# A two-layer hybrid decoder trunk: mixer gates and token shift on VectorE and ScalarE, weight tiles placed between dependent steps, and the down product's operands at another address

## The chip, the cores and the metric

The kernel runs on one core of a Trainium2 chip. The core has TensorE (PE, matrix products, with its weight loads shown apart as PEld), VectorE (DVE), ScalarE (ACT), GpSimd (POOL), and SyncE (SP), whose queue issues the DMAs here. Each engine works through its own instructions in a fixed order and waits on semaphores where an operand or a buffer is not ready. The metric is the device time of one execution in microseconds, as the median of several runs.

## The reference

Two decoder layers over 512 tokens of width 1024, float32, then a final RMSNorm. In each layer, with `n = RMSNorm(h)`:

```python
p = n @ w_in                                     # 1024 x 4256
p_rw = p_rw + (shift(p_rw) - p_rw) * mu_shift    # token shift of r, k, v, decay, iclr, gate columns
y_a = rwkv7_time_mix(p_rw) @ w_out_rwkv          # 8 heads x 64, delta-rule recurrence over tokens
y_b = mla(q_lat, kv_lat, k_pe) @ w_out_mla       # 8 heads, causal softmax, rotary key
h = h + (sigmoid(gate_a) * y_a + sigmoid(gate_b) * y_b) @ w_out
u_gate, u_val = split(RMSNorm(h) @ w_ffn_up)     # 2 x 2816
h = h + (gelu(causal_conv3(u_gate)) * u_val) @ w_ffn_down
```

The token shift takes, for each token, a mix of its own projection and the one of the token before it; for the first token the one before is zero.

## The kernel before

Activations lie with features on the 128 partitions and the 512 tokens along the free dimension. Every large product is computed to nearly float32 accuracy from two rounded parts: an operand is split into a high part (ACT, a copy that rounds) and a low part (DVE, the difference). `mm3` (lines 245 to 248) then multiplies high by high, high by low and low by high, so that a block of 128 x 128 weights takes three matmuls of 512 columns. `wtile` (line 250) makes one output tile of 128 features: eight blocks, 24 matmuls, for a product over 1024 features.

Weights come as one stream of units of eight blocks, in the order of use that `_stream` lays out on the host. `produce` loads a unit (SP), and `parts` splits it (L201 on ACT, L202 on DVE). There are two buffers each for the raw unit and its two parts, so a unit can be split only when PE is done with the unit two before it.

A layer goes through these stages:

1. *First projections.* The gate-lora and decay/iclr columns, two gate tiles (`GATES[5]`) and the lora products, `rgate_d`.
2. *Pair stage* (lines 469 to 580). `pair(p)` is a generator for two heads: it projects k, r, v (`shifted`), forms decays with a scan (L478 to L504), normalises the key (L508 to L518), builds the operands AR, BK and BKb, and computes the chunk matrices in two halves of four chunks each (L553 on PE, masked into AM by L556 on DVE; L561 transposes BKb). It yields between steps, and the loop after it runs steps of pair p, steps of pair p+1 and gate tiles in turn. PSUM holds five `m` tiles for these steps and three accumulators.
3. *Latents* of the attention (lines 597 to 625): four projections, two token sums, two inverse roots, and their broadcast to all partitions (`rsqrt_bc`: DVE, a power on POOL, a copy on ACT, four transposes on PE).
4. *A_ak V* (L633), then the *triangular inversion*: DVE transposes, 30 substitution steps of two DVE instructions (L648, L650), DVE transposes, and a join of blocks on PE (L663, L670).
5. *Chunk recurrence* (from line 677): eight chunks, each with three dependent groups of small matmuls on PE (L687, L696, L704) with DVE between them. After it in the program stand the six gates of `GATES[4]`.
6. *Attention*, the gated outputs, the merge, `w_out`, and the feed-forward part, whose up product reads operands from the `xop` pool and whose down product reads operands (`hid`) from the pool `ff`, where they lie behind seven `ft` tiles of 520 floats.

A gate tile before: ACT copies PSUM to `gg` (L433), POOL multiplies by `rstd` (L437), ACT takes tanh (L438), SP stores it to `gate_d`. A shifted tile before: POOL clears column 0 of `cur` (L417), DVE writes `cur = ps * rstd` from column 1 on (L418), POOL subtracts (L420), DVE multiplies by `mu` and adds (L421).

The order of instructions on each engine is set ahead of the run by a planner of the tile framework. It takes program order as priority, and its own estimates of durations; where it thinks an engine would wait, it draws later work forward, as far as that work's operands and its tile slots (by `tag` and `bufs`) allow. So the gates of `GATES[4]` and the attention's first projections appear in the trace within the inversion and the recurrence, though they are written behind them. Tile pools are placed one after another in SBUF, those with `side="right"` from the far end.

Of the kernel before, what the change touches and what calls it, by code (L numbers as in the profile page):

```python
# [73 lines left out]
def _blocks(w):  # L74
    """[K, M] -> [K/128 * M/128 blocks of 128 x 128], output tile by output tile."""
    k, m = w.shape
    return w.reshape(k // 128, 128, m // 128, 128).transpose(2, 0, 1, 3).reshape(-1, 128, 128)
# [10 lines left out]
GATES = (range(2, 4), range(4, 6), range(6, 8), range(8, 10), range(10, 16), range(0, 2))  # L88


# the last operands of w_out come late: its first tiles leave them to the end
# [4 lines left out]
def _stream(a, l):  # L96
    """All weights of one layer as blocks of 128 x 128 in the order of their use, 8 to a unit."""
# [11 lines left out]
    out.append(lora.reshape(128, 8, 128).transpose(1, 0, 2))  # L109
    for p in range(4):  # L110
        if p == 0:
            out.append(tiles(_W_IN_RWKV[2:5]))
        out.append(tiles(_W_IN_RWKV[5 + 3 * p:8 + 3 * p] + [_W_IN_GATE[i] for i in GATES[p]]))
# [22 lines left out]
# units of the last tile of the last product, which is taken in two halves of its tokens  # L136
# [22 lines left out]
def build(ctx, tc, x, pos, wst, vecd, constd, out):  # L159
# [36 lines left out]
    # ---- weight stream: units of 8 blocks, split into high and low parts ahead of their use  # L196
# [8 lines left out]
    def produce():  # L205
# [4 lines left out]
        if u >= NUNITS - HELD:  # L210
            # the operands' slots are free by then: these units stay
# [12 lines left out]
    class Blocks:  # L224
        """Hands out 128 x 128 weight blocks in stream order."""
# [33 lines left out]
    def split(pool, src, scale, tag, bufs=None):  # L259
        """src * scale -> exact high and low operands."""  # L260
# [16 lines left out]
    def rsqrt_bc(ps, n, eps, mul=None, out=None, pst=stat, js=range(4)):  # L277
        """ps[:, js] (sums by token, blocks of 128) -> (ps / n + eps) ** -0.5 on all partitions"""
# [5 lines left out]
        w = sm.tile([128, 512], F32, name="nw", tag="nsq", bufs=1)  # L284
        A.copy(w[:, c].rearrange("p (j n) -> p j n", n=128), v[:, 4 + a:4 + b, None].to_broadcast([128, b - a, 128]))
        pb = pst()
# [14 lines left out]
    class Norm:  # L301
        """Sums of squares over the features; add() takes them tile by tile."""
# [21 lines left out]
    # ---- rotary tables  # L324
# [23 lines left out]
    # ---- scratch in DRAM  # L348
# [6 lines left out]
    # derived vectors  # L355
    der = []

    def derive():
        for l in range(DEPTH):
            d = cp.tile([128, 24], F32, name=f"der{l}")  # L360
# [4 lines left out]
            V.tensor_scalar(d[:, 16:20], vc(l, "k_a", 0, 4), -0.5, 1.0, ALU.mult, ALU.add)  # L365
            der.append(d)
# [25 lines left out]
    def mixer(l, ops, nrm, wks):  # L392
        with ExitStack() as mx:
# [201 lines left out]
            with pool(name=f"ti{l}", bufs=2) as ti:  # L595
# [119 lines left out]
                for i in GATES[4]:  # L715
                    gate(i, ti)
# [252 lines left out]
```

## Time and profile before

| | |
|---|---|
| median of 3 runs | 1656.53 us (1648.63 to 1659.28) |
| span of the profiled execution | 1654.1 us |
| PE busy | 1593.0 us (96%), 9014 matmuls |
| DVE busy | 959.5 us (58%) |
| ACT busy | 645.2 us (39%) |
| POOL busy | 275.4 us (17%) |
| pair stage, layer 0 | 53.6 to 191.2 us |
| latents and inversion, layer 0 | 191.2 to 262.8 us |
| recurrence, layer 0 | 262.8 to 305.5 us |
| pair stage, layer 1 | 854 to 1004 us |

The profile is of one execution. The first instruction of the span starts it and the last ends it; the three runs were timed apart from it, so 1654.1 stands beside them as one more execution, 2.4 us under their median. A busy PE is not PE at its peak: matmuls overlap in the record, so their spacing is the time of a stretch without gaps over its count. A few matmul records can be missing. The stage boundaries were read from the order of PE's instructions.

### The profile page before, as it was taken

How to read it: one execution, taken by the hardware profiler on the slowest of the kernel's cores; microseconds unless marked ns; L12 is line 12 of the kernel's file. 1: busy time of each engine (PE TensorE's matmuls, PEld its weight loads, DVE VectorE, ACT ScalarE, POOL GpSimd, SP SyncE). 2: the span in 40 equal slices, each digit the busy share in tenths (PEclk: the TensorE clock that was granted, in tenths of full speed). 3: DMA queues.
4: the chain of work that ended last, by engine and by line, in shares of the span. 5: the costliest groups of instructions: out<-in, count | busy, mean ns of one | idle time of the engine just before them, and what ended most of it. 6: DMA issues, size and time to landing. Idle time of an engine off the chain costs nothing.

```text
span 1654.1 us, 22422 instructions
## 1 busy us (share of the span) xinstructions
PE 1593.0 (96%) x9014; PEld 1271.2 (77%) x9014; DVE 959.5 (58%) x1448; ACT 645.2 (39%) x987; POOL 275.4 (17%) x246
## 2 busy tenths in 40 slices
PE   8999989999999999999999998899999999999997
PEld 6877766668888888888877777766688888888886
DVE  6668885666546555533348669747565555554333
ACT  6334333573433333322234333336634433333222
POOL 2333212400211011100023332123003111110000
PEclk9999989999999999999999999899999999999998
DMA  5323312314423233233342222223244233323232
GB/s 201 111 88 104 102 65 71 116 46 136 145 90 102 90 101 97 95 110 113 108 146 96 83 83 96 71 73 95 69 141 128 88 98 95 102 89 102 90 102 78
DMA packets 57849, 166.09 MB, mean 100 GB/s; under 512 B 6416, under 2 KB 9616, under 8 KB 57744
## 3 DMA queue, kind: packets, MB, share of 16 engines
q1 hardware_dynamic: 57600, 164.48, 31.0%
q8 instruction: 71, 1.16, 0.3%
q14 instruction: 34, 0.28, 0.1%
q10 hardware_dynamic: 144, 0.16, 0.0%
HBM read 147.32 MB, written 17.30 MB: 100 GB/s over the span
## 4 chain that ended last, share of the span: by engine, by line
PE 85%; DVE 10%; issue 2%; ACT 1%; POOL 1%; DMA 1%; SPq 0%; POOLq 0%; DVEq 0%; ACTq 0%
PE acc L246 24%; PE acc L247 24%; PE acc L248 24%; DVE wlo L202 3%; PE sc L830 2%; PE po L848 2%; PE pt L841 1%; PE xy L696 1%; DVE X L644 1%; DVE tm L648 1%; DVE AM L653 1%; POOL nv L283 1%; DVE X L650 1%; PE m L553 1%; DVE z L485 1%
## 5 line engine op out<-in xcount | busy, mean ns | idle before, releaser
L246 PE MATMUL acc<-hi,whi 128*128 128x512 f32 (+1 forms) x1910 | 755.7, 396 | 5.3 <-ACT hi L267 5.3
L248 PE MATMUL acc<-hi,wlo 128*128 128x512 f32 (+1 forms) x1910 | 748.9, 392 | 1.9 <-DVE wlo L202 1.8
L247 PE MATMUL acc<-lo,whi 128*128 128x512 f32 (+1 forms) x1910 | 750.6, 393 | 0.0
L201 ACT CAST whi<-raw 128x1024 fp32r<-128x1024 f32 (+2 forms) x249 | 253.3, 1019 | 569.1 <-PE acc L247 530.5
L202 DVE TENSOR_TENSOR wlo<-raw,whi 128x1024 fp32r<-128x1024 f32 (+2 forms) x249 | 327.5, 1319 | 188.9 <-ACT whi L201 188.1
L246 PEld LDWEIGHTS acc<-hi,whi 128*128 128x128 f32 x1910 | 362.4, 190 | 82.1 <-ACT hi L267 5.3
L248 PEld LDWEIGHTS acc<-hi,wlo 128*128 128x128 f32 x1910 | 361.7, 189 | 80.6 <-DVE wlo L202 3.6
L247 PEld LDWEIGHTS acc<-lo,whi 128*128 128x128 f32 x1910 | 362.2, 190 | 74.3 <-issue 0.7
L920 POOL TENSOR_TENSOR c<-c,rstd 128x512 f32<-128x512 f32 x44 | 57.3, 1304 | 378.0 <-ACT c L919 378.0
L913 DVE TENSOR_TENSOR u<-acc,rstd 128x512 f32<-128x512 f32 x44 | 30.3, 691 | 99.9 <-PE acc L248 94.1
L922 DVE TENSOR_TENSOR c<-c,acc 128x512 f32<-128x512 f32 x44 | 30.2, 687 | 82.4 <-POOL c L920 82.4
L437 POOL TENSOR_TENSOR gg<-gg,rstd 128x512 f32<-128x512 f32 x32 | 52.0, 1625 | 121.2 <-ACT gg L433 121.2
L919 ACT ACTIVATE c<-c 128x512 f32<-128x512 f32 x44 | 27.6, 632 | 78.7 <-DVE c L918 78.7
L315 POOL TENSOR_TENSOR nacc<-nacc,nsq 128x512 f32<-128x512 f32 x14 | 25.1, 1790 | 197.6 <-ACT nsq L314 197.6
L283 POOL TENSOR_TENSOR nv<-nv,cst 128x4 f32<-128x4 f32 (+1 forms) x10 | 14.4, 1440 | 234.5 <-DVE nv L282 234.5
L418 DVE TENSOR_TENSOR cur<-acc,rstd 128x512 f32<-128x512 f32 x28 | 19.2, 691 | 47.9 <-PE acc L248 42.1
L830 PE MATMUL sc<-K,q 128*128 128x128 f32 (+3 forms) x128 | 45.3, 449 | 0.0
L836 ACT ACTIVATE P<-P,mn 128x128 f32<-128x128 f32 (+3 forms) x64 | 35.5, 556 | 16.7 <-DVE mn L833 12.9
L553 PE MATMUL m<-AR,BK 64*128 64x128 f32 x256 | 25.4, 324 | 17.3 <-DVE AM L556 17.3
L833 DVE CUSTOM_DVE_ANT_0 P<-sc,cst 128x128 f32<-128x128 f32 (+3 forms) x64 | 30.4, 482 | 16.6 <-PE pt L841 9.7
L438 ACT ACTIVATE gg<-gg 128x512 f32<-128x512 f32 x32 | 20.2, 632 | 45.4 <-POOL gg L437 45.4
L848 PEld LDWEIGHTS po<-PT,Vt 128*64 128x64 f32 x320 | 22.0, 136 | 20.7 <-issue 8.8
(232 smaller groups left out, 1499.9 us busy)
## 6 DMA issues: line engine op xcount, KB each, us to landing
raw<-in_w SPq DMA_DIRECT2D x238, 512.0 KB, 3.4
gate_d<-gg SPq DMA_DIRECT2D x32, 256.0 KB, 2.4
AM<-gate_d SPq DMA_DIRECT2D x16, 256.0 KB, 4.1
gb<-gate_d SPq DMA_DIRECT2D x16, 256.0 KB, 3.7
h<-in_x SPq DMA_DIRECT2D x8, 256.0 KB, 4.5
rgate_d<-gt SPq DMA_DIRECT2D x8, 256.0 KB, 2.6
bl_d<-rk SPq DMA_DIRECT2D x8, 256.0 KB, 2.0
bl<-bl_d SPq DMA_DIRECT2D x8, 256.0 KB, 2.7
```

What stands on the lines that cost most here:

```text
L201: A.copy(hi, r)
L202: V.tensor_tensor(lo, r, hi.bitcast(F32), ALU.subtract)
L246: PE.matmul(ps, w[0], xx[0], start=first, stop=False)
L247: PE.matmul(ps, w[0], xx[1], start=False, stop=False)
L248: PE.matmul(ps, w[1], xx[0], start=False, stop=last)
L283: G.tensor_tensor(v[:, 4 + a:4 + b], v[:, a:b], mhalf[:, a:b], ALU.pow)
L437: G.tensor_tensor(gg, gg, rstd, ALU.mult)
L553: PE.matmul(pA[hh][:, c * 128:c * 128 + 128], BK[64 * hh:64 * hh + 64, 4 * hf + c, :], AR[p][64 * hh:64 * hh + 64, 4 * hf + c, :], start=T ...
L830: PE.matmul(sp[:, 0:n], qs[hh][:, 128 * b:128 * b + 128], ks[hh][:, 0:n], start=True, stop=True)
L836: A.activation(P[:, 0:n], P[:, 0:n], AF.Exp, bias=mn[:, 0:1], scale=-1.0, accum_out=mn[:, 1:2])
L848: PE.matmul(po[64 * hh:64 * hh + 64, 128 * b:128 * b + 128], Vt[:, kb, 64 * hd:64 * hd + 64], PTs[hh][:, 128 * kb:128 * kb + 128], start=k ...
L920: G.tensor_tensor(cc, cc, rstd, ALU.mult)
```

## The change

- *Gates.* `gate` now has DVE write `gg = ps * rstd` straight from PSUM, then tanh and the store. The two early gates (`gate_raw`, `GATES[5]`) still copy on ACT, and multiply on DVE instead of POOL.
- *Token shift.* `cur` has 512 columns and no cleared one. ACT writes `o = cur * (1 - mu)`, with `1 - mu` held in 14 new columns of `der`; DVE then adds `mu * cur` of the token before to columns 1 to 511. `der` grows from 24 to 40 columns in each layer, 128 bytes for both.
- *Pair steps.* `pair` yields also behind k, and behind each half of the chunk matrices. Pair p+2's k (for p of 0 and 1) or a third gate (for p of 2 and 3) is put between the halves of pair p. `GATES` gives pairs 2 and 3 three gates instead of two, and the group of the recurrence four instead of six. `_stream` follows the new order.
- *Latents.* `rsqrt_bc` is cut into `rsqrt_tok` (through the copy on ACT) and `spread` (transposes and the final pass). Both token sums and both `rsqrt_tok` now come ahead of the A_ak V products, the two `spread` and the scaling of the key latent behind them. The copies go into tiles of their own.
- *Inversion.* One gate of `GATES[4]` is written between the substitution and the join; the other three remain behind the recurrence.
- *Feed-forward.* The `ft` tiles have 528 instead of 520 floats; the columns used are the same.

Comments and docstrings were dropped too; that part of the diff is left out.

```diff
-GATES = (range(2, 4), range(4, 6), range(6, 8), range(8, 10), range(10, 16), range(0, 2))
+GATES = (range(2, 4), range(4, 6), range(6, 9), range(9, 12), range(12, 16), range(0, 2))
...
+    out.append(tiles(_W_IN_RWKV[2:6]))
     for p in range(4):
-        if p == 0:
-            out.append(tiles(_W_IN_RWKV[2:5]))
-        out.append(tiles(_W_IN_RWKV[5 + 3 * p:8 + 3 * p] + [_W_IN_GATE[i] for i in GATES[p]]))
+        out.append(tiles(_W_IN_RWKV[6 + 3 * p:8 + 3 * p] + [_W_IN_GATE[i] for i in GATES[p]] + _W_IN_RWKV[8 + 3 * p:9 + 3 * p]))
...
     def rsqrt_bc(ps, n, eps, mul=None, out=None, pst=stat, js=range(4)):
+        return spread(rsqrt_tok(ps, n, eps, js), mul, out, pst, js)
+
+    def rsqrt_tok(ps, n, eps, js=range(4), pool=sm, tag="nsq"):
         v = sm.tile([128, 8], F32, name="nv", tag="nv", bufs=2)
         a, b = js[0], js[-1] + 1
         c = slice(128 * a, 128 * b)
         V.tensor_scalar(v[:, a:b], ps[:, a:b], 1.0 / n, eps, ALU.mult, ALU.add)
         G.tensor_tensor(v[:, 4 + a:4 + b], v[:, a:b], mhalf[:, a:b], ALU.pow)
-        w = sm.tile([128, 512], F32, name="nw", tag="nsq", bufs=1)
+        w = pool.tile([128, 512], F32, name="nw", tag=tag, bufs=1)
         A.copy(w[:, c].rearrange("p (j n) -> p j n", n=128), v[:, 4 + a:4 + b, None].to_broadcast([128, b - a, 128]))
+        return w
+
+    def spread(w, mul, out, pst, js=range(4)):
         pb = pst()
...
-            d = cp.tile([128, 24], F32, name=f"der{l}")
+            d = cp.tile([128, 40], F32, name=f"der{l}")
...
+            V.tensor_scalar(d[:, 20:34], vc(l, "mu", 0, 14), -1.0, 1.0, ALU.mult, ALU.add)
...
-                    cur = ta.tile([128, 513], F32, name="cur", tag="cur", bufs=2)
-                    G.memset(cur[:, 0:1], 0.0)
-                    V.tensor_tensor(cur[:, 1:513], ps, rstd, ALU.mult)
+                    cur = ta.tile([128, 512], F32, name="cur", tag="cur", bufs=2)
+                    V.tensor_tensor(cur, ps, rstd, ALU.mult)
                     o = ta.tile([128, 512], F32, name=name, tag="sh", bufs=6)
-                    G.tensor_tensor(o, cur[:, 0:512], cur[:, 1:513], ALU.subtract)
-                    V.scalar_tensor_tensor(o, o, vc(l, "mu", idx), cur[:, 1:513], ALU.mult, ALU.add)
+                    A.activation(o, cur, AF.Copy, scale=der[l][:, 20 + idx:21 + idx])
+                    V.scalar_tensor_tensor(o[:, 1:512], cur[:, 0:511], vc(l, "mu", idx), o[:, 1:512], ALU.mult, ALU.add)
                     return o
...
                 def gate(i, pool=ta):
-                    gate_end(i, gate_raw(pool))
+                    ps = wtile(ops)
+                    gg = pool.tile([128, 512], F32, name="gg", tag="gg", bufs=2)
+                    V.tensor_tensor(gg, ps, rstd, ALU.mult)
+                    gate_out(i, gg)
...
                 def gate_end(i, gg):
-                    G.tensor_tensor(gg, gg, rstd, ALU.mult)
+                    V.tensor_tensor(gg, gg, rstd, ALU.mult)
+                    gate_out(i, gg)
+
+                def gate_out(i, gg):
                     A.activation(gg, gg, AF.Tanh, scale=0.5)
                     nc.sync.dma_start(gate_d[i], gg)
...
                     k = shifted(2 + 3 * p, "k")
+                    yield
                     r = shifted(3 + 3 * p, "r")
...
                         A.copy(BT[p][:, 4 * hf:4 * hf + 4, :].rearrange("p c n -> p (c n)"), pB)
+                        yield
 
                 pairs = [pair(p) for p in range(4)]
-                next(pairs[0])
-                next(pairs[0])
+                for _ in range(3):
+                    next(pairs[0])
+                next(pairs[1])
                 for p in range(4):
                     if p < 3:
                         next(pairs[p + 1])
                     next(pairs[p])
-                    for i in GATES[p][:1]:
+                    gate(GATES[p][0])
+                    next(pairs[p])
+                    gate(GATES[p][1])
+                    if p < 3:
+                        next(pairs[p + 1])
+                    next(pairs[p])
+
+                    if p < 2:
+                        next(pairs[p + 2])
+                    for i in GATES[p][2:]:
                         gate(i)
                     next(pairs[p])
-                    for i in GATES[p][1:]:
-                        gate(i)
-                    if p < 3:
-                        next(pairs[p + 1])
-                    next(pairs[p], None)
...
-                ssq = sc()
-                tok_sums(ssq, sq[0])
-                rq = tl.tile([128, 512], F32, name="rq", bufs=1)
-                rsqrt_bc(ssq, 256.0, NORM_EPS, tabs[1], rq, sc)
-                ssq = sc()
-                tok_sums(ssq, sq[2])
-                rk = ti.tile([128, 512], F32, name="rk", bufs=1)
-                rsqrt_bc(ssq, 128.0, NORM_EPS, None, rk, sc)
...
+                ws = []
+                for i, (t, n) in enumerate(((sq[0], 256.0), (sq[2], 128.0))):
+                    ssq = sc()
+                    tok_sums(ssq, t)
+                    ws.append(rsqrt_tok(ssq, n, NORM_EPS, pool=ti, tag=f"nw{i}"))
...
+                rq = tl.tile([128, 512], F32, name="rq", bufs=1)
+                spread(ws[0], tabs[1], rq, sc)
+                rk = ti.tile([128, 512], F32, name="rk", bufs=1)
+                spread(ws[1], None, rk, sc)
...
+                gate(GATES[4][0], ti)
                 half = [(64, 64), (0, 128)]
...
-                for i in GATES[4]:
+                for i in GATES[4][1:]:
                     gate(i, ti)
...
-                    u = fp.tile([128, 520], F32, name="u", tag="ft", bufs=7)
+                    u = fp.tile([128, 528], F32, name="u", tag="ft", bufs=7)
...
-                    c = fp.tile([128, 520], F32, name="c", tag="ft", bufs=7)
+                    c = fp.tile([128, 528], F32, name="c", tag="ft", bufs=7)
```

More of the change, by code (lines that the diff above doesn't have):

```diff
@@ L611, in mixer @@
                 G.tensor_tensor(sq[0], sq[0], sq[1], ALU.add)
-                ssq = sc()
-                tok_sums(ssq, sq[0])
-                rq = tl.tile([128, 512], F32, name="rq", bufs=1)
-                rsqrt_bc(ssq, 256.0, NORM_EPS, tabs[1], rq, sc)
-                ssq = sc()
-                tok_sums(ssq, sq[2])
-                rk = ti.tile([128, 512], F32, name="rk", bufs=1)
-                rsqrt_bc(ssq, 128.0, NORM_EPS, None, rk, sc)
-                V.scalar_tensor_tensor(lat[2], lat[2], vc(l, "kv_norm"), rk, ALU.mult, ALU.mult)
-                kp = tl.tile([128, 512], F32, name="kp", bufs=1)
-                k2 = ti.tile([128, 512], F32, name="k2", bufs=1)
-                V.tensor_tensor(kp[64:128, :], lat[3][0:64, :], tabs[0][0:64, :], ALU.mult)
-                V.tensor_tensor(k2[64:128, :], lat[3][64:128, :], tabs[0][64:128, :], ALU.mult)
-                V.tensor_tensor(kp[64:128, :], kp[64:128, :], k2[64:128, :], ALU.add)
+                ws = []
[3 more added lines that the diff above has]
+                    ws.append(rsqrt_tok(ssq, n, NORM_EPS, pool=ti, tag=f"nw{i}"))
                 for i in range(4):
@@ L637, in mixer @@
                         A.copy(Z[ur:ur + 64, i, e, :], ps[ur:ur + 64, e, :])
+                rq = tl.tile([128, 512], F32, name="rq", bufs=1)
+                spread(ws[0], tabs[1], rq, sc)
+                rk = ti.tile([128, 512], F32, name="rk", bufs=1)
+                spread(ws[1], None, rk, sc)
+                V.scalar_tensor_tensor(lat[2], lat[2], vc(l, "kv_norm"), rk, ALU.mult, ALU.mult)
+                kp = tl.tile([128, 512], F32, name="kp", bufs=1)
+                k2 = ti.tile([128, 512], F32, name="k2", bufs=1)
+                V.tensor_tensor(kp[64:128, :], lat[3][0:64, :], tabs[0][0:64, :], ALU.mult)
+                V.tensor_tensor(k2[64:128, :], lat[3][64:128, :], tabs[0][64:128, :], ALU.mult)
+                V.tensor_tensor(kp[64:128, :], kp[64:128, :], k2[64:128, :], ALU.add)
                 X = ti.tile([128, 32, 32], F32, name="X", bufs=1)
```

## The prediction

> **What bounds the kernel now.** I read the page first, then the waits of TensorE (PE), then stretches of the span, then the order of time around one of the longest waits.
>
> ```profile
> span 1654.1 us, 22422 instructions
> ...
> PEclk9999989999999999999999999899999999999998
> ...
> PE 85%; DVE 10%; issue 2%; ACT 1%; POOL 1%; DMA 1%; SPq 0%; POOLq 0%; DVEq 0%; ACTq 0%
> ```
>
> The chain that ended last is 85% PE, so time is won only by making PE wait less, run at a higher clock, or do a matmul faster. GpSimd (POOL) holds 1% of the chain: taking work off it wins nothing by itself. The view of waits on PE, columns "us in total, times, longest us", names what holds PE up, both layers together:
>
> ```profile
> PE m L553 <- DVE AM L556: 17.3, 6, 2.9
> PE sc L288 <- ACT nw L285: 9.1, 2, 4.5
> PE xy L663 <- DVE T L655: 6.2, 4, 2.8
> ```
>
> All three lie in the mixer. Now the stretches. The columns are: stretch, length, busy us (and records) of PE, PE weight loads, VectorE (DVE), ScalarE (ACT), POOL, then the granted PE clock.
>
> ```profile
> 53.60:191.20 137.60, 128.79 (x661) 103.94 (x659) 104.57 (x123) 54.86 (x79) 47.00 (x41) 0.94 0.28 91
> 854.00:1004.00 150.00, 140.89 (x725) 113.18 (x724) 104.74 (x112) 58.18 (x83) 48.48 (x45) 0.97 0.30 98
> 89.70:95.50 5.80, 5.79 (x25) 4.99 (x26) 3.82 (x6) 3.52 (x7) 0.72 (x1) 0.50 0.16 64
> 191.20:262.80 71.60, 63.05 (x606) 50.53 (x603) 59.66 (x96) 23.45 (x35) 9.23 (x7) 0.93 0.26 85
> 262.80:305.50 42.70, 40.85 (x453) 29.72 (x452) 23.57 (x39) 13.45 (x25) 10.90 (x14) 1.00 0.25 81
> ...
> 490.00:700.00 210.00, 210.00 (x929) 173.87 (x928) 117.48 (x160) 81.64 (x102) 27.64 (x22) 1.00 0.31 98
> 724.00:825.00 101.00, 101.00 (x434) 81.15 (x433) 34.90 (x38) 26.41 (x32) 0.18 (x3) 1.00 0.35 110
> ```
>
> The first two rows are the pair stage (four head pairs, lines 481 to 580) of layer 0 and layer 1, the third the 5.8 us just after one of the L553 waits, the fourth layer 0's latents and triangular inversion, the fifth its chunk recurrence; the last two are parts of layer 0's up and down products. After the wait PE runs at clock 0.50, so a wait costs twice: as idle time and as slow matmuls. In the fourth stretch DVE is the fuller of the two dependent engines: 59.66 of 71.60 us, most of it the inversion's transposes and serial substitution. There PE's idle time is not the bound.
>
> Why does PE wait at L553? The order of time, DVE, then POOL, then PE:
>
> ```profile
> 82.28 4.07 DVE L202 TENSOR_TENSOR wlo<-raw,whi 128x1024 fp32r<-128x1024 f32 x2
> 86.27 1.53 DVE L485 TENSOR_SCALAR z<-z 128x512 f32<-128x512 f32 x1
> 87.83 1.24 DVE L488 TENSOR_TENSOR_SCAN L<-d,z 128x520 f32<-128x520 f32 x1
> 88.99 1.26 DVE L556 TENSOR_TENSOR AM<-m,cst 128x512 f32<-128x512 f32 x2
> ...
> 82.03 2.09 POOL L531 TENSOR_TENSOR BKb<-BK,z 128x1024 f32<-128x1024 f32 x1 [2.43 <-DVE BK L525]
> 85.53 1.93 POOL L437 TENSOR_TENSOR gg<-gg,rstd 128x512 f32<-128x512 f32 x1 [1.41 <-ACT gg L433]
> ...
> 86.28 0.48 PE L553 MATMUL m<-AR,BK 64*128 64x128 f32 x2
> 89.71 0.59 PE L553 MATMUL m<-AR,BK 64*128 64x128 f32 x2 [2.94 <-DVE AM L556]
> ```
>
> PE has done the first half of the chunk matrices and needs a PSUM tile back for the second. The masking (L556) that frees it stands in DVE's queue behind two weight splits, z and a scan. The splits are slow because POOL runs beside them; one without POOL beside it takes 1.21 us:
>
> ```profile
> 65.69 1.21 DVE L202 TENSOR_TENSOR wlo<-raw,whi 128x1024 fp32r<-128x1024 f32 x1
> ```
>
> **The change, part by part.** *Gates and token shift off POOL.* The rows, "busy, mean ns | idle before":
>
> ```profile
> L437 POOL TENSOR_TENSOR gg<-gg,rstd 128x512 f32<-128x512 f32 x32 | 52.0, 1625 | 121.2 <-ACT gg L433 121.2
> ...
> L418 DVE TENSOR_TENSOR cur<-acc,rstd 128x512 f32<-128x512 f32 x28 | 19.2, 691 | 47.9 <-PE acc L248 42.1 <-ACT rstd L292 5.8
> L433 ACT COPY gg<-acc 128x512 f32<-128x512 f32 x32 | 18.6, 582 | 0.5
> ...
> L932 ACT ACTIVATE h<-h,vec 128x512 f32<-128x512 f32 x7 | 5.1, 723 | 0.2
> ```
>
> 28 of the 32 gates lose the ACT copy (0.58 us) and the POOL pass (1.63 us) and gain one DVE pass of 0.69 us (L418 is the same operation and form); the other four swap POOL for DVE. The shift loses a POOL subtraction and a memset and gains an ACT scaling (0.72 us by L932); DVE keeps two passes. DVE in layer 0's pair stage gets ten evictions (6.9 us) and two more splits (2.4 us); eight gate passes of POOL, 13 us, leave it, and if half of each held DVE up, 6.5 us come back: some 3 us more on 104.57, in a stretch some 5 us shorter, so DVE remains under PE. I cost this part at nothing of its own. What hides it is the 5.4 us (24 matmuls of 226 ns, 210.00 us over 929) that each tile takes on PE; were that cover gone, each shift would show ACT's 0.72 us. On ACT the scaling queues behind the casts (L201) that wait for PE; behind it wait DVE's second pass and then the pair's chain, again with a tile of PE as cover. Gate stores go out on SP's queue earlier, so the weight loads behind them lose nothing.
>
> *The tile between the halves.* The new `yield` after each half, with a `k` projection (pairs 0 and 1) or a third gate (2 and 3) between halves, puts 24 matmuls there: 5.4 us of work where PE now waits 2.9 us. So DVE may be 2.5 us later than now before the wait returns. Gain from waits: 17.3 us, both layers. Gain from clock: time lost is (1 - clock) times length, 0.06 x 137.6 + 0.03 x 150 = 8.3 + 4.5 = 12.8 us, of which I take off 2 us that lie inside the waits themselves: 11. Together 28.3 us. What is next late here is the first half itself, which waits for BK and did not wait before.
>
> [...]
>
> *Two gate tiles per layer moved from `GATES[4]` into the pair stage.* PE's total work is the same: 48 matmuls x 226 ns = 10.9 us per layer. But they leave the stretch 191 to 305 us, where they filled PE while DVE set the pace, so that stretch does not get shorter for their leaving. If nothing takes their place, all 10.9 us per layer are lost; if attention work is drawn forward in full, none. The nearest rows are the recurrence before and after its gates run out, at 285.5 us, where attention projections take over:
>
> ```profile
> 262.80:285.50 22.70, 22.50 (x241) 16.45 (x240) 12.54 (x17) 6.00 (x10) 5.49 (x6) 1.00 0.22 71
> 285.50:305.50 20.00, 18.34 (x214) 13.27 (x212) 11.04 (x22) 7.45 (x16) 5.41 (x8) 1.00 0.28 93
> ```
>
> Without gates PE was still busy 18.34 of 20.00 us. So refilling works, but the attention's softmax also loads DVE and ACT, on which the recurrence depends. I take two thirds refilled, nearer the full end because of that row: a loss of 3.9 us per layer, 7.8 in all (ends 0 and 21.8).
>
> *Latents and inversion reordered.* Both token sums and both powers now come ahead of the A_ak V matmuls (L633), and the broadcasts behind them; `gate(12)` is written ahead of L663. The 4.5 us wait at L288 should go, but it lies beside the DVE chain, so only DVE's own waits count. In 191 to 263 us the longest of those that the reorder removes is
>
> ```profile
> DVE lat L620 <- ACT rk L292: 2.2, 1, 2.2
> ```
>
> Against it stand the gates' evictions, now on DVE, at 0.69 us each, two or three of them inside the chain. Ends: 2.2 us per layer won, 2.8 lost if all four fall there with the waits kept. I take +1.5 per layer, 3 in all, towards the upper end because the gates' POOL passes no longer collide with the chain.
>
> *Operands of the down product.* From the pool sizes: the split weights are followed by sizes that are multiples of 512 bytes, except 64 for `nv`; then 7 x 2080 bytes of `ft` make the operands start 288 past the weights mod 512. With 7 x 2112 it is 0, as for the up product. The up and the down stretch shown above have no gap in them: 226.0 and 232.7 ns a matmul (101.00 us over 434). Twelve gate-lora matmuls per layer, whose operands also lie 288 off, show the longer duration in the mean of L246 against 389 (131.51 us over 338) in the up product:
>
> ```profile
> L246 PE MATMUL m<-hi,whi 128*128 128x512 f32 x8 | 3.2, 396 | 0.0
> ...
> 490.00:720.00 230.00, 131.51 (x338) 63.24 (x337) 1.00 0.30 98
> ```
>
> So 6.7 ns x 1056 matmuls = 7.1 us; I take 6.5. The `mop` operands of w_out go from 256 off to 128, since the constants grow by 128 bytes: 384 matmuls that could lose 6.7 ns each, 2.6 us. No row shows 128; I take 0, as 0 and 256 are both fast.
>
> **Sum.** 28.3 - 7.8 + 3.0 + 6.5 = 30.0 us. The profiled execution's span is 1654.1, which becomes 1624; the median of the three runs, 1656.53, lies 2.4 above that span, so I forecast 1656.5 - 30 = 1626.5.
>
> **Rivals.**
> 1. *No refill.* The planner or the tile slots keep attention out of the recurrence, and the moved tiles are simply added: 14 us less, 1640.5. For it: attention reuses the SBUF of the inversion's tiles. Against it: the 18.34 of 20.00.
> 2. *The placement does nothing.* The slow down product has another cause: 6.5 us less, 1633. [...]
> 3. *Full refill.* All 7.8 us come back: 1619. For it: the attention of one head pair is more work than is missing.
> 4. *Slower: the recurrence starves and the clock falls there.* With no refill, PE has gaps at every dependent step, and runs the recurrence at 0.50. That doubles its 40.85 us; with half of this hidden it costs 20 us per layer, 40 in both. Sum: 28.3 - 21.8 + 3.0 + 6.5 - 40 = -24, or 1680. It decides as soon as more than 16 us of those 40 appear beside no refill. For it: layer 1's recurrence ran at clock 0.93 already:
>
> ```profile
> 1077.40:1123.00 45.60, 43.75 (x452) 31.78 (x454) 23.48 (x39) 13.38 (x25) 10.89 (x14) 0.93 0.23 76
> ```
>
> Against it: layer 0's ran at 1.00 with the same work.
>
> **Chances.** Forecast 0.48, no refill 0.16, placement nothing 0.15, full refill 0.13, slower 0.08. About 1%, here 1640.0 to 1673.1, is what a measurement of this kernel can tell from no change. Faster by more: nine tenths of the forecast (0.43), most of the placement case (0.11), all of the full refill, 0.4 of no refill (0.06): 0.73. Within: 0.19. Slower: 0.08. The range 1608 to 1648 takes the full refill with 11 us to spare for a recurrence with fewer clock drops, and no refill with 7.5 us to spare for pair waits that stay in part.
>
> **What would show it.** Right: L553 gone from PE's waits or under 3 us; clock 0.99 or more in both pair stages; that stage about 5 us shorter in layer 0 and 2 in layer 1, with two more tiles in it; L804 starting well before the recurrence's middle; the down product at 226 ns. Wrong: a wait of PE for an accumulator that DVE evicts late, ACT's scaling of the shift behind a weight cast that waits for PE, new PE waits at L687, L696 or L663 with a clock under 0.9 there, or w_out at 233 ns.

## The result, and the profile after

The changed kernel takes 1616.17 us (median of 4 runs, 1615.35 to 1616.36); the kernel before took 1655.77 beside it (1648.63 to 1659.28). The ratio is 0.977, with a 95% interval of 0.974 to 0.979: 2.3% faster. The forecast was 1626.5 with a range of 1608 to 1648, so the sign and the range held, and the gain was 10 us larger than forecast. One of the four executions of e5 below, of 4386 us, is left out of its median. The profiled execution after has a span of 1614.6 us, 39.5 under the one before.

The page of the changed kernel, its first line, the granted clock in 40 slices, and the sums of the chain that ended last:

```profile
span 1614.6 us, 22337 instructions
...
PEclk9999999999999999999999999899999999999998
...
PE 79%; issue 10%; DVE 7%; POOL 2%; ACT 1%; DMA 0%; POOLq 0%; DVEq 0%; SPq 0%; ACTq 0%
```

The slices at 8 after are one in layer 1's latents and inversion (1009 to 1049 us) and the last. Before there was one more, at 207 to 248 us, in layer 0's inversion; the drops in the pair stage are too short for this row and show only in the stretches. The waits of PE after ("us in total, times, longest us"), the four that matter here:

```profile
PE sc L294 <- ACT nw L288: 7.1, 4, 3.2
PE xy L685 <- DVE T L676: 7.1, 4, 1.9
...
PE acc L246 <- DVE gg L436: 3.1, 2, 1.5
PE xy L709 <- DVE St L735: 2.0, 2, 1.0
```

The wait between the halves of the chunk matrices (17.3 us before, at L553, now L566) is gone. A small new one has come: PE waits 3.1 us for an accumulator that DVE evicts late, as the gate's eviction (L436) is DVE's now. Now the stretches that answer to those of before; the columns are those of the prediction:

```profile
52.60:183.20 130.60, 130.60 (x709) 105.61 (x708) 97.73 (x135) 61.33 (x87) 21.23 (x14) 1.00 0.33 109
831.50:979.60 148.10, 148.10 (x786) 119.54 (x785) 97.37 (x125) 66.80 (x94) 21.01 (x14) 1.00 0.34 114
183.20:255.00 71.80, 63.01 (x599) 50.14 (x598) 61.75 (x101) 21.77 (x32) 4.10 (x3) 0.90 0.25 81
255.00:301.50 46.50, 45.22 (x487) 32.32 (x488) 27.84 (x68) 22.41 (x51) 8.62 (x13) 1.00 0.15 48
301.50:360.40 58.90, 56.60 (x532) 37.85 (x531) 40.93 (x119) 40.81 (x96) 13.15 (x11) 1.00 0.24 76
...
708.00:805.00 97.00, 97.00 (x429) 80.34 (x429) 34.08 (x37) 26.05 (x30) 0.00 (x0) 1.00 0.35 114
```

In the pair stages (first two rows) PE is busy all the time at clock 1.00, with 48 more matmuls in layer 0's. The stretches of layer 1, here and ahead of the prediction, take in pair 0's projections, some 16 us (14 us before), which those of layer 0 leave out; the table below leaves them out in both. The fourth and fifth rows are layer 0's recurrence and what is left of its attention. Before, that last stretch was

```profile
305.50:381.00 75.50, 74.84 (x625) 50.20 (x624) 49.93 (x153) 55.00 (x132) 14.79 (x13) 1.00 0.26 84
```

so 17 us of attention have moved into the recurrence, which grew by 4. How it sits there, PE in order of time within the recurrence, after:

```profile
269.80 0.39 PE L248 MATMUL acc<-hi,wlo 128*128 128x512 f32 x1
270.03 0.38 PE L852 MATMUL sc<-K,q 128*128 128x128 f32 x2
270.34 0.69 PE L726 MATMUL xy<-Z,BT 128*64 128x64 f32 x16
270.96 0.50 PE L246 MATMUL acc<-hi,lk 128*128 128x512 f32 x1
271.30 0.82 PE L852 MATMUL sc<-K,q 128*128 128x128 f32 x4
272.04 0.68 PE L709 MATMUL xy<-St,AR 64*64 64x64 f32 x16
```

Between the dependent groups (L709, L718, L726) lie the scores of the attention (L852), not only projections. That is 15 us into a recurrence that starts at 255.00. Before, the first score came 39 us into it, 3.6 us before its end at 305.50:

```profile
301.56 0.50 PE L248 MATMUL acc<-hi,wlo 128*128 128x512 f32 x1
301.90 0.27 PE L830 MATMUL sc<-K,q 128*128 128x128 f32 x1
```

Stage by stage, from the order of PE's instructions in each trace, in us ("latents to recurrence" ends with the recurrence's last matmul, "attention" is what then remains of it, "merge" holds the gated outputs, the merge and `w_out`; each pair of numbers is layer 0, layer 1; e1 and the others are the runs of the next section):

| kernel | pair stage | latents to recurrence | attention | merge | feed-forward | span |
|---|---|---|---|---|---|---|
| before | 138.7, 136.3 | 112.4, 116.9 | 76.4, 76.4 | 103.9, 103.9 | 354.5, 352.5 | 1654.1 |
| after | 131.6, 131.7 | 118.1, 117.3 | 59.1, 60.1 | 107.5, 107.5 | 351.0, 350.1 | 1614.6 |
| e1 | 135.1, 132.0 | 120.8, 119.1 | 60.3, 60.3 | 106.8, 106.8 | 350.9, 350.1 | 1624.2 |
| e2 | 130.1, 132.3 | 114.7, 117.4 | 76.5, 76.5 | 105.9, 105.9 | 354.5, 353.1 | 1648.0 |
| e4 | 131.5, 131.7 | 119.7, 120.3 | 59.1, 60.2 | 107.5, 107.5 | 351.0, 350.3 | 1620.0 |
| e5 | 137.2, 140.3 | 123.4, 124.6 | 60.3, 60.3 | 106.8, 106.8 | 351.0, 349.7 | 1640.8 |
| e6 | 126.4, 126.4 | 117.1, 114.9 | 70.8, 70.6 | 105.1, 105.2 | 351.0, 350.1 | 1618.7 |
| e7 | 142.5, 142.6 | 120.4, 119.6 | 60.3, 60.3 | 106.8, 106.8 | 351.0, 350.1 | 1641.6 |

The pair stages are 11.7 us shorter although two more tiles per layer lie in them, 10.9 us for the two; from the latents through the merge 20.3 us go in both layers together; the feed-forward parts give 5.9, and the start of the layers the rest. The merge is 3.6 us longer in each layer: ten more of its large matmuls, 2.3 us, stand behind the attention's last matmul than before (356 against 346), and `w_out`'s own matmuls have become slower, 1.3 us (see e8). Each row is one execution. How far that can be trusted shows in e3, which changes nothing in the pair stage: layer 1's is 2.7 us shorter there than in the kernel before.

### The profile page after: what moved, and what is told of

Its sections match the earlier page's. It is cut to its first block, busy times and chain, and to the rows that moved or that the text cites. A ratio compares the mean times of both kernels' runs of the same rounds, so it can differ in the third digit from the quotient of the medians.

```text
span 1614.6 us, 22337 instructions
## 1 busy us (share of the span) xinstructions
PE 1568.8 (97%) x9014; PEld 1259.1 (78%) x9014; DVE 942.0 (58%) x1482; ACT 651.0 (40%) x987; POOL 190.4 (12%) x158
## 4 chain that ended last, share of the span: by engine, by line
PE 79%; issue 10%; DVE 7%; POOL 2%; ACT 1%; DMA 0%; POOLq 0%; DVEq 0%; SPq 0%; ACTq 0%
PE acc L246 22%; PE acc L248 22%; PE acc L247 22%; PE sc L852 2%; PE po L870 2%; PE xy L718 1%; PE pt L863 1%; DVE AM L674 1%; DVE X L665 1%; DVE wlo L202 1%; POOL mu L781 1%; PE m L566 1%; DVE tm L669 1%; DVE X L671 1%; POOL nv L286 1%
## 5 line engine op out<-in xcount | busy, mean ns | idle before, releaser
L202 DVE TENSOR_TENSOR wlo<-raw,whi 128x1024 fp32r<-128x1024 f32 (+2 forms) x249 | 308.3, 1239 | 182.0 <-ACT whi L201 181.2
L858 ACT ACTIVATE P<-P,mn 128x128 f32<-128x128 f32 (+3 forms) x64 | 35.5, 556 | 26.1 <-DVE mn L855 22.8
L852 PE MATMUL sc<-K,q 128*128 128x128 f32 (+3 forms) x128 | 44.5, 447 | 0.0
L436 DVE TENSOR_TENSOR gg<-acc,rstd 128x512 f32<-128x512 f32 x28 | 19.2, 686 | 36.9 <-PE acc L248 36.7
L860 ACT ACTIVATE P<-P,mn 128x128 f32<-128x128 f32 (+3 forms) x64 | 34.8, 558 | 8.8 <-DVE mn L859 8.8
L870 PE MATMUL po<-PT,Vt 128*64 128x128 f32 x320 | 37.5, 286 | 0.8 <-DVE PT L865 0.8
L938 ACT ACTIVATE c<-u,vec 128x512 f32<-128x512 f32 x44 | 35.4, 809 | 2.3 <-DVE u L935 1.5
```

Of the source, the lines that this page charges most:

```text
L202: V.tensor_tensor(lo, r, hi.bitcast(F32), ALU.subtract)
L852: PE.matmul(sp[:, 0:n], qs[hh][:, 128 * b:128 * b + 128], ks[hh][:, 0:n], start=True, stop=True)
L858: A.activation(P[:, 0:n], P[:, 0:n], AF.Exp, bias=mn[:, 0:1], scale=-1.0, accum_out=mn[:, 1:2])
L860: A.activation(P[:, 0:n], P[:, 0:n], AF.Copy, scale=mn[:, 2:3])
L870: PE.matmul(po[64 * hh:64 * hh + 64, 128 * b:128 * b + 128], Vt[:, kb, 64 * hd:64 * hd + 64], PTs[hh][:, 128 * kb:128 * kb + 128], start=k ...
L938: A.activation(cc, u[:, 2:514], AF.Identity, bias=vc(l, "conv_b", i), scale=vc(l, "conv_w", 2 * FT + i))
```

## The experiments

Theory: the order of the work on PE (a tile between the halves, attention in place of the moved gates) carries the gain, the address of the down product's operands gives 7 us, and the engines of gates and shift give nothing alone. Rivals: that the engines carry it; that the placement does nothing; that the moved gates are lost or could be moved further.

**e1: the order without the engines.** The changed kernel with gates and shift as before.

```diff
...
-                    A.activation(o, cur, AF.Copy, scale=der[l][:, 20 + idx:21 + idx])
-                    V.scalar_tensor_tensor(o[:, 1:512], cur[:, 0:511], vc(l, "mu", idx), o[:, 1:512], ALU.mult, ALU.add)
+                    G.tensor_tensor(o, cur[:, 0:512], cur[:, 1:513], ALU.subtract)
+                    V.scalar_tensor_tensor(o, o, vc(l, "mu", idx), cur[:, 1:513], ALU.mult, ALU.add)
...
-                    V.tensor_tensor(gg, gg, rstd, ALU.mult)
+                    G.tensor_tensor(gg, gg, rstd, ALU.mult)
```

> The changed kernel with gates and token shift put back on GpSimd (old `shifted`, `gate`, `gate_end`); order of tiles, latents and placement stay new. Cover theory (the tile between the halves hides DVE's queue): PE's waits for L556's masks stay under 2 us in all, the clock in both pair stages stays at 0.99 or more, and the time is 1618 to 1626. Offload theory (the waits went because GpSimd no longer slows the weight splits): most of the waits are back, 10 us or more in all, the clock in the pair stages falls to 0.96 or less, and the time is 1635 or more.

Measured 1625.17 us, ratio 0.982 (0.979 to 0.985): 9.0 us over the changed kernel. The expectation was 1618 to 1626. PE does not wait between the halves here either, so the order covers even the slow masking. What is lost lies in layer 0's pair stage (3.5 us, of which 2.0 are a wait of PE at L524 for ACT and 0.8 one at L545 for DVE) and from the latents to the end of the attention (5.9 us in both layers, by the table).

**e2: the engines without the order.** The kernel before, with the new gates and shift.

```diff
...
-                    gate_end(i, gate_raw(pool))
+                    ps = wtile(ops)
+                    gg = pool.tile([128, 512], F32, name="gg", tag="gg", bufs=2)
+                    V.tensor_tensor(gg, ps, rstd, ALU.mult)
+                    gate_out(i, gg)
...
```

> The kernel before with only gates and token shift moved to DVE and ScalarE; order and placement old. Cover theory: in DVE's run before the masks the second split falls from about 2.0 to 1.2 us and z from 1.5 to 0.5, an eviction of 0.7 may come in, so each wait falls from 2.9 to about 1.8 us; 10 us of PE waits for the masks remain of 17.3, and the time is 1644 to 1653. Offload theory: under 5 us of these waits remain, the pair stages run at clock 0.99, and the time is 1632 or less.

Measured 1653.4 us beside 1654.2 for the kernel before, ratio 0.999 (0.9975 to 1.001): no difference that this can tell. The wait is two thirds of what it was:

```profile
PE m L559 <- DVE AM L562: 11.4, 6, 1.9
```

So the same edit is worth nothing measurable by itself and 9.0 us on top of the new order. Part of what it gives in the pair stage (8.6 us in layer 0 and 4.0 in layer 1 by the profile) is given back behind it: the stage from the latents to the recurrence is 2.3 and 0.5 us longer, the merge 2.0 in each layer (1.3 of them by `w_out`, as `der` has grown here too, see e8). The span of its profile is 6.1 us shorter, the median of its runs only 0.8: the profiled execution was the fastest of ten, 3.5 us under their median, so these stage differences flatter it.

**e3: the placement alone.** The kernel before, with `ft` tiles of 528.

> The kernel before with only the feed-forward tiles at 528 floats, so that the down product's operands lie as the weights do mod 512; w_out's operands stay 256 off. Placement theory: 226.7 ns a matmul in the down product instead of 233.3, and 7.0 us less: 1648.8. Rival (PE's reads do not meet, the slow down product has another cause): 233 ns and no change, 1655.8. w_out at 226.7 ns in both.

Measured 1645.58 us, ratio 0.995 (0.993 to 0.997): 8.6 us less than the kernel before beside it, with the expected 7.0 well inside the interval. The wait at L553 is as it was, while the same stretch of the down product holds 13 matmuls more than before's 434:

```profile
PE m L553 <- DVE AM L556: 17.3, 6, 2.9
```
```profile
724.00:825.00 101.00, 101.00 (x447) 83.65 (x446) 37.06 (x40) 28.19 (x33) 0.18 (x3) 1.00 0.33 113
```

The rival that placement does nothing falls.

**e4: the latents in the old order.** The changed kernel, each token sum followed by its own whole `rsqrt_bc` again, ahead of the A_ak V products.

```diff
-                ws = []
-                for i, (t, n) in enumerate(((sq[0], 256.0), (sq[2], 128.0))):
-                    ssq = sc()
-                    tok_sums(ssq, t)
-                    ws.append(rsqrt_tok(ssq, n, NORM_EPS, pool=ti, tag=f"nw{i}"))
+                ssq = sc()
+                tok_sums(ssq, sq[0])
+                rq = tl.tile([128, 512], F32, name="rq", bufs=1)
+                rsqrt_bc(ssq, 256.0, NORM_EPS, tabs[1], rq, sc)
...
```

> The changed kernel with the latents in the old order (each broadcast right behind its sum, ahead of the A_ak V products). If the reorder shortens DVE's serial chain: DVE waits of about 3 us per layer come back in the latents, and the time is 3 to 8 us more, 1619 to 1624. Rival (DVE's transposes and substitution set the end whatever PE does there): PE's waits at the broadcast are back at 4.5 us a layer, and the time is within 2 us of the changed kernel.

Measured 1621.66 us, ratio 0.980 (0.977 to 0.983): the reorder is worth 5.5 us. The wait for the broadcast is back at its old length,

```profile
PE sc L294 <- ACT nw L288: 9.1, 2, 4.6
```

and with it a lower clock. The same two stretches (layer 0, layer 1) of the changed kernel and then of this one:

```profile
200.00:280.00 80.00, 70.28 (x776) 53.74 (x774) 60.75 (x115) 30.05 (x54) 10.55 (x13) 0.91 0.22 74
1000.00:1090.00 90.00, 79.86 (x925) 59.91 (x924) 64.55 (x125) 35.32 (x65) 10.93 (x15) 0.94 0.18 60
```
```profile
200.00:280.00 80.00, 69.62 (x756) 54.09 (x756) 60.28 (x111) 28.80 (x50) 9.97 (x11) 0.89 0.22 73
1000.00:1090.00 90.00, 79.62 (x869) 60.61 (x868) 64.43 (x127) 34.17 (x64) 10.02 (x13) 0.89 0.19 65
```

By (1 - clock) times length that is 0.02 x 80 + 0.05 x 90 = 6.1 us more lost to the clock, as much as the whole difference. DVE's wait for the same broadcast, which the first theory of the expectation went by, comes back too, but smaller than expected: 2.2 us in each layer against 0.9 and 0.7 in the changed kernel. So the time is that of the first theory and PE's wait that of the rival; what of the 5.5 us is DVE's chain and what the clock, this run does not separate.

**e5: no tile between the halves.** The changed kernel, with the tile put behind the second half; the tiles are the same.

```diff
+                    next(pairs[p])
                     if p < 2:
                         next(pairs[p + 2])
                     for i in GATES[p][2:]:
                         gate(i)
-                    next(pairs[p])
```

> The changed kernel with the tile between the two halves of the chunk matrices moved behind the second half; engines, latents, gates and placement stay new. Cover theory: the masks' waits return at the size that the engines-only kernel showed, about 11 us in all, with 3 to 6 us of lost clock: 1630 to 1634. Rival (the planner or the shorter DVE queue hides the masks anyway): under 3 us of such waits, 1616 to 1620.

Measured 1642.85 us, ratio 0.993 (0.991 to 0.995): 27 us are lost, 9 more than the most I expected. The wait is back, and the clock falls behind it:

```profile
PE m L566 <- DVE AM L569: 11.4, 6, 1.9
```
```profile
87.53 2.06 PE L566 MATMUL m<-AR,BK 64*128 64x128 f32 x14 [1.90 <-DVE AM L569]
```
```profile
87.60:91.00 3.40, 3.40 (x20) 3.08 (x21) 2.94 (x5) 3.18 (x6) 0.72 (x1) 0.50 0.22 83
```

By the table the pair stages lose 5.6 and 8.6 us, and the stage behind them 5.3 and 7.3. But a pair stage ends in the table with its last chunk matrix, and in e5 the third gate of pair 3 stands behind that: its 24 matmuls are counted with the latents (690 matmuls in layer 0's pair stage, 714 in the changed kernel's). With this tile of 5.4 us put back, the pair stages lose 11.0 and 14.0 us, and the stage behind them changes by -0.1 and 1.9. The loss thus lies almost whole where the tile was moved. The two pair stages of e5 as the table has them:

```profile
51.40:188.40 137.00, 130.81 (x690) 105.63 (x689) 98.18 (x134) 60.86 (x85) 20.31 (x14) 0.98 0.29 98
859.10:999.20 140.10, 133.94 (x690) 107.82 (x689) 88.99 (x114) 58.17 (x82) 21.54 (x14) 0.95 0.26 91
```

Of the 25 us the waits for the masks are 11.4, as expected. The clock, 1.00 in the changed kernel, takes 0.02 x 137.0 + 0.05 x 140.1 = 9.7, where 3 to 6 were expected. The other 4 us are not accounted for.

**e6: one gate back to the recurrence.**

```diff
-GATES = (range(2, 4), range(4, 6), range(6, 9), range(9, 12), range(12, 16), range(0, 2))
+GATES = (range(2, 4), range(4, 6), range(6, 9), range(9, 11), range(11, 16), range(0, 2))
```

> The changed kernel with one gate tile per layer given back from the pair stage (pair 3 has two gates, no tile between its halves) to the recurrence's group (five). Refill theory (attention work takes the place of any gate that leaves the recurrence): the pair stages get 5.4 us shorter each, and what follows up to the up product 5.4 us longer, so the time stays within 3 us of the changed kernel. Rival (what leaves the recurrence is lost): 8 to 11 us faster than the changed kernel, 1605 to 1608.

Measured 1620.97 us, ratio 0.980 (0.978 to 0.981). The pair stages are 5.2 and 5.3 us shorter, a tile each; the remaining attention is 11.7 and 10.5 longer, as less of it is drawn in. Were a moved gate lost, this would have been 8 to 11 us faster than the changed kernel; it is 4.8 slower, so that it also misses the 3 us within which the refill theory wanted it. The clock from the latents to the recurrence is 0.93 and 0.94 here against 0.94 and 0.96, some 3.3 us by (1 - clock) times length, and that may be why. So the place of this one gate, the second of the two that were moved, is refilled in full when it leaves the recurrence; the first was not tested.

**e7: two more gates moved.** Three gates in every pair, two left for the recurrence.

```diff
-GATES = (range(2, 4), range(4, 6), range(6, 9), range(9, 12), range(12, 16), range(0, 2))
+GATES = (range(2, 5), range(5, 8), range(8, 11), range(11, 14), range(14, 16), range(0, 2))
...
```

> The changed kernel with two more gate tiles per layer moved into the pair stage (three per pair, two left in the recurrence's group). Refill theory: pair stages 10.9 us longer each, the rest 10.9 us shorter, time within 4 us of the changed kernel, unless PE runs dry ahead of the inversion's join, where attention work cannot go because its tiles lie in the inversion's memory: then 5 to 12 us slower. Rival (nothing refills): 22 us slower, 1638.

Measured 1643.07 us, ratio 0.993 (0.992 to 0.995): 27 us over the changed kernel, more than either side of the expectation had. The pair stages grow by the two tiles (10.9 us each), and what remains of the attention is no shorter. The waits of the inversion's join, and two stretches from there into the recurrence:

```profile
PE xy L686 <- DVE T L677: 20.1, 4, 5.2
...
PE xy L693 <- DVE Q L689: 5.6, 4, 1.4
```
```profile
247.80:275.10 27.30, 14.52 (x295) 12.16 (x296) 13.17 (x12) 5.49 (x9) 0.00 (x0) 0.50 0.07 23
1056.70:1084.00 27.30, 13.93 (x294) 11.68 (x294) 13.41 (x11) 5.17 (x9) 0.00 (x0) 0.50 0.09 33
```

PE runs dry ahead of the join and then stands at half clock for 27.3 us in each layer, and is busy for 14.5 and 13.9 of them. In the changed kernel the join's wait (L685) was 7.1 us. The 13.0 us by which it grew and half of the 28.4 us that PE is busy at half clock, 14.2, make about the 27 us by this estimate. So the refill has an end between four gates left and two.

**e8: the operands of `w_out` at 0.**

```diff
-            d = cp.tile([128, 40], F32, name=f"der{l}")
+            d = cp.tile([128, 56], F32, name=f"der{l}")
```

> The changed kernel with the derived vectors padded to 56 columns, which moves the weights by 128 bytes more, so that w_out's operands lie 0 off the weights mod 512 and the down product's still 0. Placement theory: w_out at 226.7 ns a matmul instead of 233.3, 384 x 6.6 ns = 2.5 us less: 1613.6. Rival (w_out became slow for another reason of the new order): unchanged, 1616.

Measured 1614.04 us (1613.59 to 1614.34), ratio 0.9754 (0.9736 to 0.9771): faster than both kernels, and 2.1 us under the changed one. 40 us of `w_out` in the kernel before, the changed one and this one:

```profile
420.00:460.00 40.00, 40.00 (x178) 33.14 (x177) 21.06 (x24) 17.15 (x23) 10.68 (x6) 1.00 0.42 136
```
```profile
400.00:440.00 40.00, 40.00 (x173) 32.15 (x173) 21.24 (x23) 15.85 (x22) 9.90 (x6) 1.00 0.41 132
```
```profile
400.00:440.00 40.00, 40.00 (x178) 33.12 (x177) 20.89 (x23) 15.60 (x21) 10.69 (x6) 1.00 0.43 143
```

The fields 178, 173, 178 are the matmuls that fit into 40 us, for operands that lie, by the pool sizes, 256, 128 and 0 bytes past the weights mod 512. The merge of e8 is 1.3 us shorter in each layer than the changed kernel's.

**e9 and e10: other distances for the down product**, by the width of the `ft` tiles in layers 0 and 1.

```diff
-                    u = fp.tile([128, 528], F32, name="u", tag="ft", bufs=7)
+                    u = fp.tile([128, (592, 640)[l]], F32, name="u", tag="ft", bufs=7)    # e9
+                    u = fp.tile([128, (584, 560)[l]], F32, name="u", tag="ft", bufs=7)    # e10
...
```

> The changed kernel, with the ft tiles 592 floats wide in layer 0 and 640 in layer 1 (the columns used are the same), so that the down product's operands lie 256 bytes past the weights mod 512 in layer 0 and 64 in layer 1; in the changed kernel both are at 0 and a matmul of the down product takes 226.7 ns, in the kernel before both are at 288 and it takes 233.3. If only the distance mod 512 decides, and 0 and 256 are the fast values (as w_out's operands showed with 226.7 at 256 and 233.3 at 128): layer 0 stays at 226.7, layer 1 goes to 233.3, and its feed-forward part is 3.5 us longer (528 matmuls by 6.6 ns). If multiples of 64 were fast and 128 slow for a reason of its own: both at 226.7. If equality alone were fast and w_out's case another: both at 233.3.

> The same with widths of 584 in layer 0 and 560 in layer 1: the down product's operands lie 32 and 384 bytes past the weights mod 512. If 0 and 256 are the fast values: both layers at 233.3 ns a matmul, each feed-forward part 3.5 us longer than in the changed kernel, some 1621 to 1623 us in all. If the nearness to the weights' place decided (32 near, 384 far): layer 0 faster than layer 1, with values between 226.7 and 233.3.

Measured 1616.85 and 1621.17 us, beside 1655.38 for the kernel before (one time each). Stretches of the down product in layers 0 and 1, first of the changed kernel, then of e9, then of e10:

```profile
710.00:790.00 80.00, 80.00 (x355) 66.26 (x354) 28.34 (x30) 21.82 (x25) 0.00 (x0) 1.00 0.34 115
1480.00:1580.00 100.00, 100.00 (x443) 82.81 (x442) 32.20 (x34) 29.17 (x36) 1.29 (x1) 1.00 0.31 101
```
```profile
710.00:790.00 80.00, 80.00 (x354) 66.25 (x353) 28.21 (x30) 21.83 (x25) 0.00 (x0) 1.00 0.33 114
1480.00:1580.00 100.00, 100.00 (x438) 82.05 (x437) 31.96 (x33) 28.53 (x34) 1.07 (x1) 1.00 0.29 98
```
```profile
710.00:790.00 80.00, 80.00 (x344) 64.27 (x343) 27.23 (x29) 20.72 (x24) 0.00 (x0) 1.00 0.33 115
1480.00:1580.00 100.00, 100.00 (x431) 80.53 (x430) 31.57 (x33) 28.71 (x34) 1.29 (x1) 1.00 0.27 95
```

The mean gap between matmul starts in these stretches is 226.7 ns at 0 and at 256, 228.9 at 64, 233.3 at 32 and 233.1 at 384. That 0 and 256 are the fast distances held; that there are only two values did not, as 64 lies between.

## Why the prediction was right, and where it was off

Its sum, 30.0 us, held no term for the engines. The kernel with all but the engines, e1, has a span of 1624.2, 29.9 under before: what the forecast counted came out as counted in sum (smaller errors cancel in it), and most of its distance to the result is the one term taken as nothing. Term by term:

| step | forecast, us | runs, us |
|---|---|---|
| gates and shift off POOL | 0 | +9.0 (e1 against the changed kernel); not measurable alone (e2) |
| tile between the halves | +28.3 | +29.7 (e1); 25 lost in the pair stages without it (e5) |
| gate tiles moved, loss after refill | -7.8 | -9.0 (e1) as a remainder; -4.5 with the engines |
| latents and inversion | +3.0 | +5.5 (e4) |
| down product's operands | +6.5 | +5.9 to +7.0 |
| `w_out`'s operands | 0 | -2.5; e8 got 2.1 back |

*Gates and shift: mis-sized.* The step let half of POOL's gate passes come back on DVE and ended at 3 us more on DVE's 104.57 in layer 0's pair stage. Measured are 97.73, 6.8 us less with two more tiles to serve. It left out the subtractions of the shift: POOL's busy time there fell by 25.8 us (47.00 to 21.23), not by the 13 of the gates. With 6.9 us of new evictions and 3.0 for the two more splits in the 97.73, DVE got back 16.7 us, where the step had 6.5. About half of what came back on DVE is in the weight splits; DVE's groups in that stage, before and after ("busy, mean ns | idle before"):

```profile
L202 DVE TENSOR_TENSOR wlo<-raw,whi 128x1024 fp32r<-128x1024 f32 x18 | 34.2, 1916 | 0.5 <-ACT whi L201 0.5
...
L520 DVE TENSOR_TENSOR AR<-q,z 128x512 f32<-128x512 f32 x4 | 7.0, 1758 | 0.0
```
```profile
L202 DVE TENSOR_TENSOR wlo<-raw,whi 128x1024 fp32r<-128x1024 f32 x20 | 29.5, 1476 | 1.2 <-ACT whi L201 1.2
...
L533 DVE TENSOR_TENSOR AR<-q,z 128x512 f32<-128x512 f32 x4 | 2.7, 668 | 0.0
```

Two splits more take 4.7 us less, AR 4.3 less and z (L485, now L498) 3.2 less. In e1, with POOL's passes back, a split takes 1886 ns again. So a split is longer where POOL is busier in that stage, 1916 ns beside 47.00 us of POOL and 1476 beside 21.23. The prediction's row of 1.21 us was not a split without POOL: the subtraction L420 started 0.16 us behind it, at 65.85, and it was that one which took 1.95 us. Over the whole trace before, the 44 splits of this size that start while POOL runs take 1984 ns in the mean, the 35 beside which POOL starts later 1220, and the 156 without POOL 1224.

PE as the bound was right, so the edit by itself gave nothing (e2). Wrong was to take the term of the first edit without the second: behind the new order e1 loses 3.8 us in the pair stages and 5.9 from there to the end of the attention. The later part goes with the clock. From the end of the pair stage to that of the recurrence, layers 0 and 1, the changed kernel and then e1:

```profile
183.00:301.10 118.10, 108.04 (x1084) 82.33 (x1082) 89.65 (x168) 43.78 (x81) 12.72 (x16) 0.94 0.20 67
979.30:1096.70 117.40, 106.93 (x1084) 81.42 (x1083) 89.72 (x168) 43.88 (x81) 12.72 (x16) 0.96 0.21 68
```
```profile
187.20:308.10 120.90, 111.08 (x1089) 84.61 (x1086) 89.95 (x167) 47.31 (x88) 20.72 (x21) 0.92 0.20 66
987.60:1106.80 119.20, 110.84 (x1089) 84.08 (x1087) 90.04 (x167) 47.42 (x88) 20.58 (x21) 0.91 0.20 67
```

By (1 - clock) times length e1 loses 20.4 us there against 11.8, part of it where PE waits anyway. Which of the passes starts it was not tested, nor the gates apart from the shift.

*Tile between the halves: right.* Waits and clock went as the step said: L566 no longer waits, the clock is 1.00, and the pair stages of e1 are 7.9 us shorter with 21.8 us of tiles added. e5 confirms it from the other side: without the tile 11.4 us of waits and 9.7 us of clock return. BK, named as the next to be late, was not.

*Moved tiles: mis-sized.* Two thirds were taken as refilled, nearer the full end for the row of 18.34 busy of 20.00 us. From the latents through the merge 20.3 us went, in place of the moved 21.8; with +5.5 for the latents and -2.5 for `w_out` in it, 4.5 are lost: four fifths were refilled. The condition for more, which the step had as a doubt, "the attention's softmax also loads DVE and ACT", does not show as a limit: DVE was busy 27.84 of 46.50 us in the new recurrence. The 4.5 is a remainder and was not measured apart; e6 shows the refill, e7 its end.

*Latents: right in sign, mis-sized.* The step held that the wait for the broadcast, L288, lies beside DVE's chain and that only DVE's waits count, 2.2 us at most. DVE's wait did shrink, by 1.3 and 1.5 us in the two layers (e4), or 2.8 us in all, close to the 3.0 of the step. Measured are 5.5. PE's own wait (3.2 us at the longest after, 4.6 with the old order) carries a price of 6.1 us in clock, which the step left out (the two add up to more than the 5.5, so they overlap): it forgot in this stage what its own rows of the pair stage had shown, 5.8 us at clock 0.50 behind a wait of 2.94 us.

*Down product: right.* 6.6 ns by 1056 matmuls is 7.0 us; the feed-forward parts are 5.9 shorter, e3's 6.3. *`w_out`: the step that failed.* "No row shows 128; I take 0, as 0 and 256 are both fast" was a guess between two ends, and the upper one (2.6 us) was right: 128 is as slow as 288, 233.3 ns a matmul at both. Of the signs that the prediction named for being wrong, this one appeared, and one more: PE's 3.1 us of waits for accumulators that DVE evicts late.

The rivals. *No refill* did not happen: 1640.5 forecast, and e6 speaks against it directly. *Placement does nothing* falls by e3 and e9, e10; the lora row was read rightly. With nothing changed but the width of the `ft` tiles, the same 101 us of the down product hold 434 matmuls before and 447 in e3. *Full refill*, 1619, came nearest, but by its number only: four fifths were refilled, and the rest of its distance is made up by the engines and the latents. *Slower, the recurrence starves* did not occur in the changed kernel, but its mechanism is real and near: e7 shows it two gates further on, at 54.6 us of half clock in both layers. There it begins ahead of the inversion's join and not in the recurrence. Its point of decision was given in us of loss; a count of the gates left ahead of the join would have said more.

## What to carry to other kernels

An edit that frees an engine off the critical path may read as nothing alone and as several us behind another edit that made the order tight, so measure such parts in both orders before one is dropped. Filler work for a stage of dependent steps has a price per place, not per tile: move it to a place where PE waits, as long as other work refills the old place, and stop before PE runs dry ahead of a join: in e7 half clock followed for 27.3 us in each layer. After any change of a buffer's size, read the spacing of matmuls in every product: here 128 bytes of constants took a matmul of `w_out` from 226.7 to 233.3 ns and cost 2 us, and another 128 gave them back.

## What the runs showed of the hardware

**Operand distance.** In these runs the spacing of the 512-column matmuls, each with its own weight load (443 and 442 in 100 us of the changed kernel's down product), went with the distance between moving operand and weights in SBUF: 226.7 ns at 0 and 256 bytes mod 512, 228.9 at 64, 233.3 at 32, 128, 288 and 384 (233.1 at the last). The distances are the author's estimate, worked out from the sizes of the pools; the traces hold no addresses. They are taken mod 512 as in the prediction; no run shows that period, and the times fit mod 256 as well. By the same sizes it is the distance, not the place of one operand: `w_out`'s operands keep their address while the weights move by 128 bytes (173 matmuls in 40 us after, 178 in e8), and in e9 and e10 the weights keep theirs while the down product's operands move (226.7 ns in the changed kernel, 228.9 in layer 1 of e9, 233.3 and 233.1 in e10). Why 64 lies between is open.

**Clock.** PE's clock stood at 0.50 from 87.60 to 91.00 us in e5, right behind a wait of 1.90 us, and at 1.00 in the same stretch of the changed kernel:

```profile
87.60:91.00 3.40, 3.40 (x20) 2.60 (x20) 2.28 (x5) 3.40 (x7) 0.72 (x1) 1.00 0.32 122
```

In the kernel before it stood at 0.50 for 6.8 us (88.7 to 95.5 us, begun within the wait of 2.94 that ends at 89.7), in e7 for 27.3 in each layer. How long a wait has to be for a drop, and what sets the length of one, was not shown.

The kernel before spreads from execution to execution, and its mean clock with it. Of the 19 beside e1, the fastest took 1648.56 us at a mean clock of 0.985 and the slowest 1659.55 at 0.978; 0.007 x 1654 is 11.6 us, and they differ by 11.0. The four of the changed kernel, whose profile has clock 1.00 in both pair stages, lie within 1.0 us, at 0.989 and 0.990.
